# One more level inside two of the seven block products of a SwiGLU up-projection

## The chip, the cores and the metric

The kernel runs on one core of a Trainium2 chip. The metric is the device time in microseconds (us) of one execution, as a median of runs. The page and the trace of the profile come from one profiled execution. Times inside the trace are counted from the first instruction of that execution.

## What is computed

Two layers of a streaming encoder run over 1024 prompt tokens and 32 sample tokens, 1056 together, with 1024 features. Each layer is a mixer with its output projection, then a SwiGLU, then a gated embedding. The part that matters here is the SwiGLU with 2816 hidden features:

```python
def swiglu(x, w1, w3, w2):
    return (jax.nn.silu(x @ w1) * (x @ w3)) @ w2
...
        x = layer_norm(DEEPNORM_ALPHA * x + mix, w['ln1_g'][i], w['ln1_b'][i])
        x = layer_norm(DEEPNORM_ALPHA * x + swiglu(x, w['w_ff1'][i], w['w_ff3'][i], w['w_ff2'][i]),
                       w['ln2_g'][i], w['ln2_b'][i])
        x = x + (ple[i] @ w['w_ple'][i]) * jax.nn.sigmoid(x @ w['w_ple_gate'][i])
```

Everything is float32. A product of two float32 operands is made of three TensorE passes: each operand is split into a high part and a rest (`Weights.split`: ScalarE writes the high part, L88, VectorE the rest, L89), and high by high, rest by high and high by rest are added in PSUM.

## The kernel before

Per layer, `tail` makes the output projection, the first layer norm and group 0 of the hidden features. `up` (L899) makes groups 1 to 10. `final` (L1174) multiplies by w2, and `embed` follows.

A group is 256 hidden features, which is two tiles of 128 columns of w1 and of w3. In `up` each of these two weight matrices is taken as 2 by 2 blocks (feature half by output tile), the activations as 2 by 2 blocks (feature half by token half, 528 tokens), and the product is made by seven block products of sums instead of eight (Winograd's form of Strassen's method). `ops` names the seven activation operands: 1, 2, 3 and 4 lie in the tiles xh and xl, and 5, 6, 7 are the tiles t1, t2, t3, all of them split. Operand 4 is made in place. One block product (`product`, L980) is 4 feature tiles by 3 passes by 2 token quarters, so 24 matmuls of 128 by 128 weights on 264 columns (L989).

`quad` (L1021) runs the seven products of one weight matrix and group in the order 1, 2, 6, 5, 7, 3, 4, in tiles `q` of two PSUM banks each, four of them. ScalarE copies out a first result (`copy`, L1005), VectorE adds later ones onto it (`add`, L1008), `act` applies Silu on ScalarE (L1019) or multiplies by the gate on VectorE (L1017), and `keep` (L895) sends the hidden group to DRAM. Group 1 goes by another order that is not touched.

The weights come through the class `Weights`, a generator in the order of use: SyncE issues the load of a raw tile (L79, two buffers), VectorE makes the sums (`sub`, L94), and each item is split into half of a tile `w` (four buffers). `get` hands out an item and then has the next ones made, until four units are ahead. The instructions are put in order for each engine by a scheduler from that program order.

At the end of `up` the operand tiles are reused for the operands of `final`: hidden blocks and w2. `behind` loads t2 after product 6 of the last matrix, t3 and t1 after its product 7, and the rest, into xh and xl too, is loaded when `final` begins (L1108, L1111). `final` runs seven products again, in the order 1, 7, 6, 4, 5, 2, 3. Each runs over the 11 groups j with 24 matmuls per j (L1202), and from product 7 on it needs sums that VectorE makes in place (L1147). The residual, the tile `stream`, lies in SBUF all the while. It is read by `block_sums` at the start of `up` and written by `final` when its product 1 ends (L1212).

## Time and profile before

| what | before |
|---|---|
| median of three runs | 2317.38 us (2315.13 to 2317.8) |
| time of the profiled execution | 2315.55 us |
| span of its trace | 2313.8 us |
| mean granted TensorE clock | 0.997 of full speed |
| TensorE matmul, weight load | 99%, 98% of the span |
| VectorE, ScalarE | 68%, 43% of the span |

The time of the profiled execution is its span and 1.75 us around it. Busy shares are means over all stages, and the stages differ. Matmul ends are modelled, so a share near 100% says that the engine never ran dry and not how fast it was.

### The profile page before, as it was taken

The page shows a single profiled execution, that of the slowest core. Times are in us where ns is not written, and L with a number is a line of the kernel's source. Part 1 is how long each engine was busy: PE and PEld are TensorE (multiplying, and loading weights), DVE is VectorE, ACT ScalarE, POOL GpSimd, SP SyncE. Part 2 cuts the span into 40 slices and gives each one's busy share as a digit, 9 for nine tenths or more (in the row PEclk, how much of TensorE's full clock was granted, in tenths as well). Part 3 has the DMA queues.
Part 4 walks back from the last instruction along what each step waited for, and adds up shares of the span by engine and source line. Part 5 has one row for each costly group of instructions (what it writes and reads, how often), then busy time and mean ns, then how long its engine had stood idle before and what let it go on. Part 6 is the DMA issues. An engine that isn't in the chain of part 4 may idle for free.

```text
span 2313.8 us, 40696 instructions
## 1 busy us (share of the span) xinstructions
PE 2290.7 (99%) x17375; PEld 2257.9 (98%) x17375; DVE 1572.1 (68%) x2436; ACT 1001.5 (43%) x1671; POOL 32.4 (1%) x40
## 2 busy tenths in 40 slices
PE   9999999999999999999999999999999999999998
PEld 8999999999999999999999989899999999999998
DVE  8755797555544878896556774898455554978893
ACT  5432464333333443584543562464333333444582
POOL 0000000000000000000000120000000000000000
PEclk9999999999999999999999999999999999999999
DMA  4113113222223722034212222023221224621132
GB/s 149 48 56 123 44 59 117 69 89 74 84 74 133 252 79 70 28 104 145 74 38 66 92 81 67 27 74 109 85 74 66 93 74 159 238 86 42 47 99 95
DMA packets 84377, 207.35 MB, mean 90 GB/s; under 512 B 10236, under 2 KB 19652, under 8 KB 84196
## 3 DMA queue, kind: packets, MB, share of 16 engines
q1 hardware_dynamic: 83428, 204.07, 26.5%
q8 instruction: 136, 2.23, 0.4%
q10 hardware_dynamic: 768, 0.68, 0.1%
q14 instruction: 45, 0.37, 0.0%
HBM read 171.57 MB, written 33.16 MB: 88 GB/s over the span
## 4 chain that ended last, share of the span: by engine, by line
PE 91%; DVE 5%; DMA 2%; ACT 1%; issue 1%; POOL 0%; SPq 0%; ACTq 0%; POOLq 0%
PE q L989 37%; PE q L1202 20%; PE q L1330 8%; PE mm L228 6%; PE mm L229 6%; PE mm L230 6%; PE q L1309 2%; PE mm L638 1%; PE mm L639 1%; PE mm L640 1%; DVE bf L94 1%; DMA raw<-w 1%; DVE w L89 1%; PE ms L774 1%; DMA raw<-w_out 1%
## 5 line engine op out<-in xcount | busy, mean ns | idle before, releaser
L1202 PE MATMUL q<-w 128*128 128x264 f32 x3696 | 457.5, 285 | 0.0
L1202 PEld LDWEIGHTS q<-w 128*128 128x128 f32 x3696 | 456.4, 188 | 0.3
L88 ACT ACTIVATE w<-raw 128x512 fp32r<-128x512 f32 (+2 forms) x246 | 185.8, 774 | 223.8 <-issue 76.6
L989 PE MATMUL q<-xhin,w 128*128 128x264 f32 x1664 | 270.9, 284 | 0.6 <-ACT u L392 0.6
L89 DVE TENSOR_TENSOR w<-raw,w 128x512 fp32r<-128x512 f32 (+2 forms) x246 | 213.1, 881 | 54.5 <-ACT w L88 54.2
L89 DVE TENSOR_TENSOR w<-bf,w 128x512 fp32r<-128x512 f32 (+1 forms) x250 | 167.2, 692 | 107.3 <-ACT w L88 106.5
L88 ACT ACTIVATE w<-bf 128x512 fp32r<-128x512 f32 (+1 forms) x250 | 148.4, 628 | 196.9 <-PE q L989 79.5
L989 PEld LDWEIGHTS q<-xhin,w 128*128 128x128 f32 x1664 | 230.3, 188 | 1.2 <-ACT u L392 0.8
L989 PE MATMUL q<-xhgate,w 128*128 128x264 f32 x1280 | 207.8, 284 | 0.5 <-ACT xhgate L962 0.5
L228 PE MATMUL mm<-xhgate,w 128*128 128x384 f32 (+1 forms) x576 | 188.7, 328 | 5.4 <-ACT xhgate L322 4.7
L229 PE MATMUL mm<-xhgate,w 128*128 128x384 f32 (+1 forms) x576 | 187.6, 326 | 0.0
L230 PE MATMUL mm<-xlgate,w 128*128 128x384 f32 (+1 forms) x576 | 186.7, 325 | 0.8 <-DVE xlgate L323 0.8
L989 PEld LDWEIGHTS q<-xhgate,w 128*128 128x128 f32 x1280 | 177.2, 188 | 0.7 <-ACT xhgate L962 0.7
L989 PE MATMUL q<-xlin,w 128*128 128x264 f32 x832 | 169.6, 285 | 0.3 <-DVE xlin L963 0.3
L1330 PE MATMUL q<-xhgate,w 128*128 128x264 f32 x1024 | 167.1, 285 | 0.0
L1330 PEld LDWEIGHTS q<-xhgate,w 128*128 128x128 f32 x1024 | 142.0, 188 | 0.3
L228 PE MATMUL mm<-xhin,w 128*128 128x384 f32 (+1 forms) x384 | 127.1, 332 | 6.3 <-ACT xhin L322 5.5
L989 PE MATMUL q<-xlgate,w 128*128 128x264 f32 x640 | 130.0, 285 | 0.3 <-DVE xlgate L963 0.3
L989 PEld LDWEIGHTS q<-xlin,w 128*128 128x128 f32 x832 | 128.8, 188 | 0.7 <-DVE xlin L963 0.5
L229 PE MATMUL mm<-xhin,w 128*128 128x384 f32 (+1 forms) x384 | 125.4, 327 | 0.6 <-DVE w L89 0.6
L230 PE MATMUL mm<-xlin,w 128*128 128x384 f32 (+1 forms) x384 | 125.0, 327 | 0.1
L989 PE MATMUL q<-t2sum,w 128*128 128x264 f32 x960 | 124.2, 285 | 0.0
(333 smaller groups left out, 4215.1 us busy)
## 6 DMA issues: line engine op xcount, KB each, us to landing
raw<-w SPq DMA_DIRECT2D x116, 512.0 KB, 3.6
hidden<-c SPq DMA_DIRECT2D x44, 528.0 KB, 3.0
raw<-w_gate SPq DMA_DIRECT2D x32, 512.0 KB, 3.6
raw<-w_in SPq DMA_DIRECT2D x16, 512.0 KB, 3.8
raw<-w_out SPq DMA_DIRECT2D x16, 512.0 KB, 3.6
xhdown<-hidden SPq DMA_DIRECT2D x12, 528.0 KB, 7.8
t2down<-hidden SPq DMA_DIRECT2D x8, 528.0 KB, 3.8
t3down<-hidden SPq DMA_DIRECT2D x8, 528.0 KB, 3.7
```

The costliest lines, as they stand in the source:

```text
L88: self.nc.scalar.activation(hi, x, AF.Copy)
L89: self.nc.vector.tensor_tensor(lo, x, hi.bitcast(F32), op=ALU.subtract)
L94: self.nc.vector.tensor_tensor(t, a, b, op=op)
L228: nc.tensor.matmul(ps, wh, xh, start=first, stop=False)
L229: nc.tensor.matmul(ps, wl, xh, start=False, stop=False)
L230: nc.tensor.matmul(ps, wh, xl, start=False, stop=last)
L638: nc.tensor.matmul(o, xh, hi[:, s], start=k == 0, stop=False)
L639: nc.tensor.matmul(o, xh, lo[:, s], start=False, stop=False)
L989: nc.tensor.matmul(ps[:, a, :TH // 2], w[q][:, ks], x[r][:, k, a * TH // 2:(a + 1) * TH // 2], start=not add and k == 0 and j == 0, stop=k ...
L1202: nc.tensor.matmul(ps[m][:, a, :TH // 2], v[q][:, ms], x[r][:, a * TH // 2:(a + 1) * TH // 2], start=j == 0 and n == 0, stop=j == NG - 1 a ...
L1309: nc.tensor.matmul(ps[:, b, :TH // 2], w[q][:, o:o + P], pe[k][r][:, t * TH + b * TH // 2:t * TH + (b + 1) * TH // 2], start=k == 0 and i ...
L1330: nc.tensor.matmul(ps[:, b, :TH // 2], w[q][:, ks], token_half((self.xh, self.xl), k, t, b)[r], start=k == 0 and i == 0, stop=k == KD - 1 ...
```

## The change

In groups 3 to 10 of both layers the products 2 and 4 are no longer made for w1 and w3 apart. The two weight blocks that multiply the same operand, one of w1 and one of w3, are taken side by side as one matrix of 256 columns, and this product goes by one more level of the same seven-product form. Its blocks are 2 feature tiles by 128 columns by 264 tokens, and a product of the inner level (`one`) is 2 by 3 passes, so 6 matmuls of 264 columns. The inner level of product 2 runs within the w1 matrix of a group and that of product 4 within the w3 matrix, in four pieces between the outer products (`within`, `some`). Their results are added to the hidden tiles in pieces of 264 columns.

The outer order becomes 1, inner, 5, 6, 3, 7 in these groups, and 1, 2, 5, 6, 3, 7, 4 in group 2. The weight sums of the inner level are made from a load of its own (`_inner`). Its activation sums are made once per layer, in eight steps that are spread over the last matrix of group 2 and the first of group 3 (`inner`). They lie in the place of `stream`. So `stream` is written to DRAM when `up` begins and read back when it ends. In `up`, PSUM has three tiles `q` and two single banks, `ia` and `ib`. The hidden group goes to DRAM block by block (`keep_block`). `product` is cut in two (`blocks` holds the matmuls) without a change to them.

```diff
@@ -35,6 +35,8 @@
...
+INNER = (2, 4)
...
+            elif kind == "set":
+                yield from self._set(key, *src)
...
+    def _set(self, key, src, order, inner):
+        r0, r1 = (self.raw(v) for v in src)
+        a11, a12, a21, a22 = (r[:, h * 512:(h + 1) * 512] for r in (r0, r1) for h in range(2))
+        sums = {}
+        for i in order:
+            if i == "in":
+                yield from self._inner(*inner)
+                continue
+            if callable(i):
+                i()
+                continue
+            if i == 5:
+                sums[5] = self.sub(a21, a22, ALU.add)
+            elif i == 6:
+                sums[6] = self.sub(sums[5], a11)
+            elif i == 3:
+                sums[3] = self.sub(a12, sums[6])
+            elif i == 7:
+                sums[7] = self.sub(a11, a21)
+            x = {1: a11, 2: a12, 4: a22}.get(i)
+            yield key + (i,), 1, self.split(self.half(), sums[i] if x is None else x)
...
+    def _inner(self, key, src):
+        nc, (raw, own), rest = self.nc, self.extra, self.rest
+        for i, v in enumerate(src):
+            nc.sync.dma_start(out=raw[:, i, :], in_=v)
+        a11, a12, a21, a22 = (raw[:, i, h * 256:(h + 1) * 256] for i in range(2) for h in range(2))
+        x, y = self.temp(512), self.temp(512)
+        s1, s2, s3, s4 = (v[:, h * 256:(h + 1) * 256] for v in (x, y) for h in range(2))
+        for out, a, b, op in (
+            (s1, a21, a22, ALU.add), (s2, s1, a11, ALU.subtract), (s3, a11, a21, ALU.subtract),
+            (s4, a12, s2, ALU.subtract),
+        ):
+            nc.vector.tensor_tensor(out, a, b, op=op)
+        def place():
+            return self.place()[:, :, 0:1024].rearrange("p q (i c) -> p q i c", i=2)
+        own = own if key[3] == INNER[0] else place()
+        self.split(own.rearrange("p q i c -> p q (i c)"), raw.rearrange("p i c -> p (i c)"))
+        sum_ = place()
+        for i, v in enumerate((x, y)):
+            self.split(sum_[:, :, i, :], v)
+        self.rest = rest
+        cut = lambda t, i, h: [t[:, q, i, h * 256:(h + 1) * 256] for q in range(2)]
+        yield key, 2, {
+            1: cut(own, 0, 0), 2: cut(own, 0, 1), 4: cut(own, 1, 1),
+            5: cut(sum_, 0, 0), 6: cut(sum_, 0, 1), 7: cut(sum_, 1, 0), 3: cut(sum_, 1, 1),
+        }
...
-def plan(a, steps, ple):
+def levels(w, g):
+    j = 2 if w == 1 else 4
+    if j not in INNER or g == 2:
+        j = None
+    forms = [1, *(["in"] if j else [2] * (g == 2 or 2 not in INNER)), 5, 6, 3, 7]
+    if 2 not in INNER and "in" in forms:
+        forms.insert(1, 2)
+    if g == 2 or 4 not in INNER:
+        forms.append(4)
+    for i, at in ((2, (3, 2)), (4, (1, 3))):
+        if i in INNER and at == (w, g):
+            for n, f in enumerate((5, 6, 3, 7)):
+                forms.insert(forms.index(f) + 1, (i, n))
+    return j, forms
...
         for g in range(2, NG):
-            blocks("all", g)
+            for w in (1, 3):
+                j, forms = levels(w, g)
+                src = None
+                if j:
+                    o = [a[f"w{v}_{layer}"][2 * g + (j == 4)][:, 512:1024] for v in (1, 3)]
+                    src = ("in", layer, g, j), o
+                forms = [i if i == "in" or type(i) is int else (lambda i=i, layer=layer: inner(layer, *i)) for i in forms]
+                order.append(("set", (layer, w, g), ([a[f"w{w}_{layer}"][2 * g + i] for i in range(2)], forms, src)))
...
                     self.tp = stack.enter_context(tc.tile_pool(name=f"t{layer}", bufs=1, reuse_waits="tile"))
+                    with tc.tile_pool(name=f"psu{layer}", bufs=1, space=PSUM, reuse_waits="tile") as self.psum:
+                        self.psum_bufs = {"q": 3, "ia": 1, "ib": 1}
+                        self.up(layer)
                     self.psum = stack.enter_context(
                         tc.tile_pool(name=f"psb{layer}", bufs=1, space=PSUM, reuse_waits="tile")
                     )
                     self.psum_bufs = {"q": 4}
-                    self.up(layer)
                     self.final(layer)
                     self.embed(layer)
...
         self.begin(layer)
+        for k in range(0, KD, 2):
+            nc.sync.dma_start(out=self.resid[:, k:k + 2, :], in_=self.stream[:, k:k + 2, :])
         last = self.block_sums(self.stream, t1, t2, t3, t4)
...
+        self.inside, self.sh = {}, [self.pair(t, layer, "all") for t in "sc"]
         for g in range(2, NG):
-            s = self.pair("s", layer, g)
-            self.quad((layer, 1, g), s, None, AF.Silu)
-            h = self.pair("c", layer, g)
-            self.quad((layer, 3, g), h, s, step=behind if g == NG - 1 else None)
-            self.keep(layer, g, h)
+            for w in (1, 3):
+                self.mixed(layer, w, g, behind if (w, g) == (3, NG - 1) else None)
+        self.stream = self.const.tile([P, KD, T], F32, tag="stream", name=f"stream{layer}b", bufs=1)
+        self.acc = [self.stream[:, :, t0:t0 + n] for t0, n in CH]
+        for k in range(0, KD, 2):
+            nc.sync.dma_start(out=self.stream[:, k:k + 2, :], in_=self.resid[:, k:k + 2, :])
+    def inner(self, layer, i, step):
+        nc, w, q, x = self.nc, self.w, TH // 2, self.ops[i]
+        if not self.inside:
+            t = self.inner_sums = self.const.tile([P, 32, q], F32R, tag="stream", name=f"inner{layer}", bufs=1)
+            raw = self.tp.tile([P, 1024], F32, tag="rawx", name=f"rawx{layer}", bufs=1)
+            own = t[:, 24:32, :].rearrange("p (q b) t -> p q (b t)", q=2)[:, :, 0:1024]
+            w.extra = raw.rearrange("p (i c) -> p i c", i=2), own.rearrange("p q (i c) -> p q i c", i=2)
+        if step == 0:
+            n, t = INNER.index(i), self.inner_sums
+            t1, t2, t3 = (
+                [t[:, 12 * n + 4 * j + 2 * r:12 * n + 4 * j + 2 * r + 2, :] for r in range(2)] for j in range(3)
+            )
+            own = [[v[:, k:k + 2, h * q:(h + 1) * q] for v in x] for k in (0, 2) for h in range(2)]
+            self.inside[i] = {1: own[0], 2: own[2], 3: own[3], 4: own[1], 5: t1, 6: t2, 7: t3}
+        of = self.inside[i]
+        b11, b12, b21, b22, t1, t2, t3 = (of[n] for n in (1, 4, 2, 3, 5, 6, 7))
+        out, terms = (
+            (t3, (b22, b12, ALU.subtract)), (t2, (t3, b11, ALU.add)), (t1, (b12, b11, ALU.subtract)),
+            (b12, (b21, t2, ALU.subtract)),
+        )[step]
+        u, v, op = terms
+        s = w.temp(TH).rearrange("p (k t) -> p k t", k=2)
+        nc.vector.tensor_tensor(s, u[0].bitcast(F32), v[0].bitcast(F32), op=op)
+        nc.vector.tensor_tensor(s, s, u[1].bitcast(F32), op=ALU.add)
+        nc.vector.tensor_tensor(s, s, v[1].bitcast(F32), op=op)
+        nc.scalar.activation(out[0], s, AF.Copy)
+        nc.vector.tensor_tensor(out[1], s, out[0].bitcast(F32), op=ALU.subtract)
...
+    def mixed(self, layer, w, g, behind):
+        dst, (s, h) = self.sh[w == 3], self.sh
+        gate, func = (None, AF.Silu) if w == 1 else (s, AF.Copy)
+        j, forms = levels(w, g)
+        todo = iter(self.within(layer, j, g)) if j else iter(())
+        two, four = 2 not in forms, 4 not in forms
+        def made(i, ps=None):
+            if behind:
+                self.w.ahead = min(self.w.AHEAD, len(forms) - 1 - forms.index(i)) if i in (5, 6) else self.w.AHEAD
+            (v,) = self.w.get((layer, w, g, i))
+            ps, add = (self.quads(), False) if ps is None else (ps, True)
+            self.blocks(ps, v, self.ops[i], add)
+            if behind:
+                behind(i)
+            return ps
+        def some():
+            next(todo, None)
+        def finish(at, ps=None):
+            self.act(dst, at, gate, func, ps)
+            if w == 3:
+                self.keep_block(layer, g, at)
+        u = made(1)
+        if two and w == 3:
+            self.add(dst, (0, 0), u)
+            finish((0, 0))
+        else:
+            self.copy(dst, (0, 0), u)
+        if not two:
+            self.add(dst, (0, 0), made(2))
+            finish((0, 0))
+        some()
+        v = made(5)
+        self.copy(dst, (1, 1), v)
+        some()
+        made(6, u)
+        self.copy(dst, (0, 1), u)
+        some()
+        made(3, v)
+        self.add(dst, (0, 1), v)
+        finish((0, 1))
+        some()
+        if j:
+            self.act(s, {2: (0, 0), 4: (1, 0)}[j], None)
+        made(7, u)
+        self.add(dst, (1, 1), u)
+        finish((1, 1))
+        if not four:
+            made(4, u)
+            finish((1, 0), u)
+        elif w == 1:
+            self.copy(dst, (1, 0), u)
+        else:
+            self.add(dst, (1, 0), u)
+            finish((1, 0))
...
+    def within(self, layer, j, g):
+        nc, q, d, x = self.nc, TH // 2, self.sh, self.inside[j]
+        m, t = {2: (0, 0), 4: (1, 0)}[j]
+        (w,) = self.w.get(("in", layer, g, j))
+        def bank(tag):
+            return self.bank(tag)[:, :q]
+        def one(ps, i, add):
+            for k in range(2):
+                for c, (p, r) in enumerate(((0, 0), (1, 0), (0, 1))):
+                    nc.tensor.matmul(
+                        ps, w[i][p][:, k * P:(k + 1) * P], x[i][r][:, k, :],
+                        start=not add and k == 0 and c == 0, stop=k == 1 and c == 2, skip_group_check=add,
+                    )
+            self.passed(6 * q)
+        def to(a, b, ps, new=False):
+            o = d[a][:, m, t * TH + b * q:t * TH + (b + 1) * q]
+            if new:
+                nc.scalar.activation(o, ps, AF.Copy)
+            else:
+                nc.vector.tensor_tensor(o, o, ps, op=ALU.add)
+        u = bank("ia")
+        one(u, 1, False)
+        to(0, 0, u)
+        v = bank("ib")
+        one(v, 2, False)
+        to(0, 0, v)
+        yield
+        v = bank("ib")
+        one(v, 5, False)
+        to(1, 1, v, True)
+        one(u, 6, True)
+        to(0, 1, u)
+        yield
+        one(v, 3, True)
+        to(0, 1, v)
+        one(u, 7, True)
+        to(1, 1, u)
+        yield
+        one(u, 4, True)
+        to(1, 0, u, True)
+        yield
...
+    def keep_block(self, layer, g, at):
+        m, t = at
+        self.nc.sync.dma_start(
+            out=self.hidden[layer][:, m, t, g, :], in_=self.sh[1][:, m, t * TH:(t + 1) * TH]
+        )
```

## Rows read from the trace of the kernel before

**Rows 1.** The page's first part: busy time, share of the span and instructions.
```profile
span 2313.8 us, 40696 instructions
PE 2290.7 (99%) x17375; PEld 2257.9 (98%) x17375; DVE 1572.1 (68%) x2436; ACT 1001.5 (43%) x1671; POOL 32.4 (1%) x40
```
**Rows 2.** The chain of waits from 340 to 860 us: start, length, what.
```profile
353.85 4.24 DMA raw<-w
...
360.75 1.20 DVE w L89 x2
361.95 1.23 DVE s L1008 x2
...
377.36 372.42 PE q L989 x3049
749.78 110.23 PE q L1202 x894
```
**Rows 3.** Windows: length, busy us and instructions of each engine, PEclk, DMA share, GB/s.
```profile
360.00:370.00 10.00, 10.00 (x84) 10.00 (x84) 10.00 (x18) 4.47 (x8) 0.00 (x0) 1.00 0.33 104
...
379.50:749.50 370.00, 370.00 (x3033) 370.00 (x3032) 189.34 (x294) 127.27 (x220) 0.00 (x0) 1.00 0.27 88
749.50:784.00 34.50, 34.50 (x282) 34.50 (x281) 26.06 (x42) 15.13 (x27) 0.00 (x0) 1.00 0.97 354
784.00:846.00 62.00, 62.00 (x505) 62.00 (x504) 50.70 (x83) 26.24 (x46) 0.00 (x0) 1.00 0.31 102
...
1589.00:1958.70 369.70, 369.70 (x3031) 369.70 (x3030) 188.92 (x293) 126.89 (x219) 0.00 (x0) 1.00 0.26 88
```
**Rows 4.** Waits of TensorE from 1548 to 2055 us: total, times, longest.
```profile
PE q L989 <- ACT xhgate L962: 0.5, 1, 0.5
PE q L989 <- DVE xlgate L963: 0.3, 1, 0.3
```
**Rows 5.** VectorE's groups from 461 to 502 us, one group of hidden features.
```profile
L89 DVE TENSOR_TENSOR w<-bf,w 128x512 fp32r<-128x512 f32 x8 | 5.3, 689 | 5.1 <-ACT w L88 5.0
L89 DVE TENSOR_TENSOR w<-raw,w 128x512 fp32r<-128x512 f32 x6 | 4.0, 686 | 0.0
L1017 DVE TENSOR_TENSOR c<-c,s 128x528 f32<-128x528 f32 x4 | 2.8, 706 | 0.1
...
L94 DVE TENSOR_TENSOR bf<-raw 128x512 f32<-128x512 f32 x2 | 1.4, 693 | 7.2 <-DMA raw<-w 7.2
```
**Rows 6.** VectorE's timeline from 330 to 385 us: start, length, instruction.
```profile
339.26 0.45 DVE L885 TENSOR_TENSOR c<-c,mm 128x288 f32<-128x288 f32 x1
339.63 1.94 DVE L94 TENSOR_TENSOR bf<-stream 128x528 f32<-128x528 f32 x3
```
**Rows 7.** Windows of 5 us at the end of `up` and the start of `final`.
```profile
755.00:760.00 5.00, 5.00 (x43) 5.00 (x42) 3.18 (x6) 3.36 (x6) 0.00 (x0) 1.00 0.80 286
...
775.00:780.00 5.00, 5.00 (x43) 5.00 (x42) 4.96 (x9) 1.78 (x3) 0.00 (x0) 1.00 1.05 395
...
785.00:790.00 5.00, 5.00 (x43) 5.00 (x42) 4.79 (x9) 2.22 (x4) 0.00 (x0) 1.00 0.00 0
```
**Rows 8.** SyncE's queue in the timeline, 690 to 1020 us.
```profile
738.08 0.38 SPq L1108 DMA_DIRECT2D t2down<-hidden  x1
...
743.96 0.37 SPq L1108 DMA_DIRECT2D t3down<-hidden  x1
...
749.34 1.59 SPq L895 DMA_DIRECT2D hidden<-c  x2
750.98 0.52 SPq L1111 DMA_DIRECT2D t1down<-w  x1
758.18 0.33 SPq L1111 DMA_DIRECT2D t1down<-hidden  x1
758.61 0.90 SPq L1108 DMA_DIRECT2D xhdown<-hidden  x2
```
**Rows 9.** VectorE's timeline from 736 to 800 us.
```profile
749.82 0.71 DVE L1017 TENSOR_TENSOR c<-q,s 128x528 f32<-128x528 f32 x1 [0.52 <-PE q L989]
...
764.60 1.33 DVE L1147 TENSOR_TENSOR xhdown<-xhdown 128x528 f32<-128x528 f32 x2 [0.97 <-DMA xhdown<-hidden]
```

More of the change, by code (lines that the diff above doesn't have):

```diff
@@ L59, in __init__ @@
     def __init__(self, nc, pool, order):
-        self.nc, self.pool, self.count, self.rest = nc, pool, 0, None
+        self.nc, self.pool, self.count, self.rest, self.ahead = nc, pool, 0, None, self.AHEAD
         self.made, self.items, self.temps, self.temp_bufs = [], self._make(order), None, 5
@@ L74, in half, with raw_place @@
         return t
+    def raw_place(self):
+        self.count += 1
+        return self.pool.tile([P, T], F32, tag="raw", name=f"raw{self.count}", bufs=2)
     def raw(self, src):
-        self.count += 1
-        raw = self.pool.tile([P, T], F32, tag="raw", name=f"raw{self.count}", bufs=2)[:, :src.shape[1]]
+        raw = self.raw_place()[:, :src.shape[1]]
         self.nc.sync.dma_start(out=raw, in_=src)
@@ L127, in _make, with prefetch @@
                 yield own(a22)
-    def prefetch(self, n=AHEAD):
+    def _set(self, key, src, order, inner):
[44 more added lines that the diff above has]
+        }
+    def prefetch(self, n=None):
+        n = self.ahead if n is None else n
         while sum(m[1] for m in self.made) < n:
@@ L145, in get, with plan @@
         return out
-def plan(a, steps, ple):
+def levels(w, g):
[12 more added lines that the diff above has]
+    return j, forms
+def plan(a, steps, ple, inner):
     order = []
@@ L255, in build @@
             ring = ctx.enter_context(tc.tile_pool(name="ring", bufs=1, side="right"))
-            self.w = Weights(nc, ring, plan(a, self.steps, self.ple))
+            self.w = Weights(nc, ring, plan(a, self.steps, self.ple, self.inner))
             self.const = const
@@ L292, in build @@
             self.spill = dram.tile([P, KD, T], F32, name="spill")
+            self.resid = dram.tile([P, KD, T], F32, name="resid")
             self.acd = dram.tile([72, P], F32, name="acd")
@@ L980, in product, with blocks @@
     def product(self, key, i, ps=None):
-        nc, x = self.nc, self.ops[i]
         (w,), add = self.w.get(key), ps is not None
         ps = ps if add else self.quads()
+        self.blocks(ps, w, self.ops[i], add)
+        return ps
+    def blocks(self, ps, w, x, add):
+        nc = self.nc
         for k in range(4):
@@ L993, in product @@
         self.passed(12 * TH)
-        return ps
     @staticmethod
```

## The prediction

> **What bounds the kernel now.** I read the page's busy line first. TensorE and its weight loads are busy nearly all the time, VectorE two thirds and ScalarE under half [rows 1]. A busy TensorE on the page only means that it never ran dry, so I looked for what the end hangs on, in the chain of waits. Around the change it has two long pieces that are TensorE alone: 372.42 us for 3049 matmuls of `up` and 110.23 us for 894 of `final` [rows 2]. That is 0.1222 and 0.1233 us for one matmul of 264 columns. The waits of TensorE over the second layer's `up` and half of its `final` come to 0.8 us [rows 4]. So in this stretch a matmul left out is time left out, as long as the other engines still deliver.
>
> They have room of different size. In the windows by stage, groups 2 to 10 show VectorE busy 189.34 of 370.00 us and ScalarE 127.27 [rows 3]: 51% and 34%. The second layer repeats this within half a per cent [rows 3]. Ahead of this stretch the chain runs over VectorE and loads of raw weights [rows 2], and there a window shows VectorE busy 10.00 of 10.00 us while TensorE does all its 84 matmuls [rows 3]. So VectorE can be packed full for some ten us without hurting TensorE, but has nothing left there. The third thing to see is the DMA: from the end of `up` to 784 us it is busy 97% of the time at 354 GB/s [rows 3], at best 395 GB/s, and it falls to nothing only after 785 us [rows 7].
>
> **What is removed.** Two outer products in w1 and two in w3 are 4 x 24 = 96 matmuls in a group. Two inner products of seven times 6 matmuls are 84. So 12 matmuls less for each of 8 groups and 2 layers, 192 in all. They have the shape of those that stay, and each of them loads a weight tile of its own before and after, so the price is the one of the chain: 192 x 0.1222 = **23.5 us**. The Trainium skill, "TensorE: Matmul & The Clock Gate", section "Back-to-back issue gap", gives columns over 2.4 GHz and 2.5 ns, which is an estimate of 112.5 ns here and would make it 21.6 us. The chain shows 9% more for a matmul, and the sum keeps that.
>
> **VectorE in a group.** Instructions of 512 and 528 columns follow each other in 0.60 to 0.62 us [rows 2], one of 288 columns from PSUM in 0.37 us (339.26 to 339.63) [rows 6]. By the line through these, 256 or 264 columns cost 0.34 and 1024 about 1.12. A group has now 14 splits, 8 sums, 6 additions from PSUM and 4 gate products, 32 instructions or about 19.5 us. The window shows 189.34 / 9 = 21.0 us [rows 3], 1.08 times that. After the change there are 10 outer splits, 2 of 1024 and 4 of 512 for the inner level, 8 sums of 512 and 8 of 256, 6 + 10 additions (the 10 of half width), 4 gate products: 6.0 + 4.6 + 4.8 + 2.7 + 3.7 + 3.4 + 2.5 = 27.7 us, times 1.08 = 30 us. TensorE's group shrinks from 41.1 to 324 x 0.1222 = 39.6 us, so VectorE goes from 51% to 76%. ScalarE, at 127.27 / 220 = 0.58 us each, goes from 24 to about 32 instructions a group, under half busy. Both are hidden behind TensorE as means. A rule speaks against the small additions: the Trainium skill, "VectorE: DVE Perf Modes", section "The TRN2 errata", gives 120 cycles and the columns at 0.96 GHz for an operand from PSUM, so an estimate of 0.40 us for 264 columns. By that the group would be 0.6 us more. The 288-column row shows 0.37, and either way 76% hardly moves.
>
> What can be lost is in the order. VectorE's idle time in a group is mostly waiting: 7.2 us on two loads of raw weights and 5.0 on ScalarE [rows 5]. The inner level adds a second load, issued behind the first, and such a wait holds the additions queued behind it. The single bank `ib` is read by VectorE after one inner product and written again after one outer product, 24 x 0.1222 = 2.9 us later. A wait of 3.6 us (half of the 7.2) standing ahead of that addition would cost TensorE up to 3.6 + 0.34 - 2.9 = 1.0 us, in up to 32 matrices. Bounds 0 to 32 us. Nearest to it are the packed stretch and the waits [rows 3, 4], where TensorE lost under a microsecond. I take 1 us for both layers.
>
> **The start of `up`.** Writing `stream` out is 8 x 1056 x 128 x 4 bytes = 4.33 MB, 11 to 12 us of DMA at 395 to 354 GB/s [rows 3, 7]. It goes ahead of raw weights on SyncE's queue, and the chain has such a load at 353.85 us, 4.24 us long [rows 2]. But `stream` is final before the block sums that read it at 339.63 us [rows 6], and the DMA share in the window at 360 us is 0.33 [rows 3], so the write should be over when that load comes. 0 to 3 us a layer, taken 0.5.
>
> **Group 2 and the activation sums.** Eight steps of four VectorE instructions are 8 x 4 x 0.615 = 20 us of VectorE in two matrices that last 40 us, on top of about 23 us. Full, but group 2's first matrix still has idle time before it. If VectorE falls behind, TensorE waits as far as the slack of some 3 us is used up: 0 to 5 us a layer, taken 1. In group 2 product 4 follows product 7 into the same bank, and VectorE's addition stands between. Such an addition starts 0.04 us after the matmuls of a product end (749.78 to 749.82) and lasts 0.71 [rows 2, 9], so 0.75 us, twice a layer. Another matrix's product may fill it. 0 to 1.5, taken 1.
>
> **The end of `up`.** Here the 4.33 MB come back, into a stretch where the DMA is full. Three things move. First, product 7 was third from the end and is now last, so the loads of t3 and t1, issued from 743.96 us, 5.8 us before the change to `final` at 749.78 [rows 2, 8], wait for the end of `up`. The loads of t2 come after product 6, which now has 24 + 24 + 18 matmuls behind it, so 8.1 us before the end where it was 11.7 (738.08) [rows 8]. Second, the read back takes 11 to 12 us. Third, something is gained: the queue stood from 751.5 to 758.18 us on the load of a hidden block that `keep` had only issued at 749.34 [rows 8], and block by block that one is written early.
>
> Two orders are possible on SyncE. If the read back goes as soon as its place is free (the inner sums are last used ahead of product 3, 54 matmuls or 6.6 us before the end), it fills the DMA until about +9 us, counted from the end of `up`. The first pair of blocks and weights in t3, 1.06 MB at 354 to 395 GB/s, lands at about +12, and after 2.5 us of splits (8 instructions on two engines) serves j = 4 at +14.5. TensorE wants that at 4 x 2.93 = +11.7: a stall of **3 us**. If the loads of t3 and t1 go first, 3.2 MB and the read back end near +20, then come a rest of 0.8 MB and 1.6 MB for the first pair of product 7, landing at +26. VectorE then has eight instructions for it and four evacuations of product 1, 7.4 us, so +33.4 against product 7's start at 264 x 0.1222 = +32.3. Before, the first of these sums started at 764.60 us, +14.8 [rows 9], so this cover of 17 us is what the read back eats. A stall of 0 to 3 us. Bounds: 0 if the queue overlaps better, 12 if all of the read back is paid. I take 3 us a layer, and 0.5 for the start of `final` with its later t2 loads (0 to 3).
>
> The Trainium skill, "DMA: Bandwidth & Descriptors", section "Specifications", gives a limit of about 358 GB/s for HBM and one core. By that the read back is an estimate of 12.1 us, and the stall 1 us longer. The best window shows 395 GB/s [rows 7], which is above that limit.
>
> **The sum.** Losses a layer: 0.5 + 1 + 1 + 3 + 0.5 = 6, and 1 in the groups: 13 us for both layers. 23.5 - 13 = 10.5 us less. The profiled execution took 2315.55 us, which gives 2305. The median of the runs stands 1.8 us above it, so I predict **2306 us** for the median. Its own range, with half or one and a half of the losses, is 2300 to 2313.
>
> **Rivals.** *Nearly everything is hidden*: the losses stay under 4 us, and the time is 2294 to 2299. For it speaks that TensorE lost under 1 us where VectorE was full [rows 3, 4]; against it that the DMA has no idle time at the end of `up` to hide 4.33 MB [rows 7].
>
> *The read back is paid*: both layers lose 10 to 12 us at the change to `final`, the gain is gone, and the time is 2313 to 2321. For it speaks the full DMA, against it the 17 us of cover before product 7.
>
> *VectorE comes to set the pace in the groups*, which ends on the other side: waits on loads and on ScalarE stay (12.2 us of a group [rows 5]) and come on top of 30 us of work, 42.2 us against TensorE's 39.6. Sixteen groups at 2.6 us are 42 us, so 42 - 23.5 = some 18 us slower, 2335, and 2325 to 2345 around it. It decides from 10.5 / 32 = 0.33 us of stall a matrix. Against it: these waits come mostly from VectorE being early, and shrink when it is busy.
>
> That the matmuls aren't saved is excluded by the count.
>
> **Chances.** Forecast 45%, nearly all hidden 24%, read back paid 15%, VectorE at the pace 16%. A measurement of this kernel can tell about 0.2%, here 4.6 us, from no change, so faster is below 2312.7. The forecast lies there but for some 3 points, the first rival altogether, the second with 2 points: 68% faster. The same is 3 + 12 = 15%, and slower 1 + 16 = 17%. The range of 8 in 10 takes in the first three cases and the near part of the fourth, 2294 to 2325.
>
> **What would show it.** Right: 17183 matmuls on the page; windows of a group of 39.6 to 40.5 us with VectorE at 70 to 80%; TensorE's waits short and near the start of `final`, on ScalarE's splits of t3 or VectorE's sums; DMA full until about 45 us past `up`. Wrong: waits of TensorE on inner additions in every group (VectorE at the pace), or a single gap of 8 us and more before product 7 or j = 4 (read back paid), or none at all (hidden). The prediction falls with the ready times at the end of `up`, which hang on an order on SyncE that the trace before cannot show.

## The result and the profile after

The changed kernel takes 2303.08 us (median of 6 runs, 2300.83 to 2303.82) where the kernel before took 2317.59 beside it (6 runs, 2315.13 to 2319.16). The ratio is 0.9937, interval 0.9927 to 0.9947: 14.5 us less, where 11 were forecast. A second series of the same kernel, told below with the experiments, gives 2297.34 beside 2316.82 before, ratio 0.9916, interval 0.9899 to 0.9932, 19.5 us less. Both intervals lie wholly below 1, and they overlap each other.

The page's first part, against [rows 1]:

```profile
span 2298.6 us, 41143 instructions
...
PE 2270.4 (99%) x17183; PEld 2236.8 (97%) x17183; DVE 1736.9 (76%) x2820; ACT 1060.7 (46%) x1783; POOL 32.5 (1%) x40
```

The 192 matmuls are gone, and yet the count of all instructions is 447 higher. VectorE has 384 more and went from 68% to 76% of the span. TensorE is still the engine that never rests. Windows of the changed kernel, columns as in [rows 3]; the first is one group of hidden features, the others lie at the start of `final`:

```profile
467.10:506.70 39.60, 39.60 (x327) 39.60 (x326) 28.66 (x53) 16.77 (x30) 0.00 (x0) 1.00 0.33 109
742.00:747.00 5.00, 3.74 (x19) 3.77 (x20) 4.79 (x8) 1.15 (x2) 0.00 (x0) 0.67 0.95 330
...
777.00:782.00 5.00, 5.00 (x43) 5.00 (x42) 4.83 (x9) 3.20 (x6) 0.00 (x0) 1.00 0.96 368
782.00:787.00 5.00, 5.00 (x43) 5.00 (x42) 5.00 (x9) 2.39 (x5) 0.00 (x0) 1.00 0.06 22
1942.00:1947.00 5.00, 3.73 (x30) 3.76 (x31) 4.80 (x8) 1.15 (x2) 0.00 (x0) 1.00 0.96 301
```

From the first matmul of a group to that of the next are 39.55 us, where it was 41.01 (both counted in the traces). That is 1.46 us less, or 23.4 us in the sixteen groups. TensorE is busy throughout, and VectorE at 72%. The DMA stays full until 782 us, 39 us past the start of `final` at 743.26. Something is lost at that start: TensorE is busy for 3.74 of 5.00 us, and its granted clock falls to 0.67 in layer 0 and not at all in layer 1. All waits of TensorE over `up` and half of `final`, layer 0 (320 to 860 us) and then layer 1 (1500 to 2060 us), against [rows 4]; L1448 is `final`, L1236 an outer product of `up`:

```profile
PE q L1448 <- DVE c_all L1254: 2.2, 1, 2.2
PE q L1236 <- DVE xlin L1205: 0.2, 1, 0.2
...
PE q L1448 <- ACT w L93: 2.1, 1, 2.1
PE q L1236 <- DVE xlgate L1205: 0.3, 1, 0.3
...
PE q L1236 <- DVE c_all L1254: 0.2, 1, 0.2
```

There is one wait of some 2 us a layer, and the others are of 0.2 to 0.3 us, near the start of `up`. The chain of waits puts the long one at the first matmul of `final` in both layers (start, length, what):

```profile
733.02 4.79 DMA t2down<-hidden
737.84 1.18 ACT w L93 x2
...
741.89 1.24 DVE c_all L1254 x2
743.26 116.76 PE q L1448 x933
...
1934.55 7.47 DMA t2down<-w
...
1942.04 1.16 ACT w L93 x2
...
1943.27 116.76 PE q L1448 x945
```

In layer 0 the last thing waited for is VectorE's addition, in layer 1 ScalarE's split of a tile of t2. There the additions end at 1943.12 and the split at 1943.20, so both stand in the way.

Where the time came from is read stage by stage, from the first matmul of each stage to that of the next (us, worked out from the starts in the three traces; the last column is the same changed kernel in the second series):

| stretch | before | changed | changed, again |
|---|---|---|---|
| start to the first matmul of the convolution's projections | 58.8 | 61.3 | 59.7 |
| from there to `up` | 280.2 | 280.2 | 279.5 |
| `up`, layer 0 | 410.6 | 401.8 | 401.8 |
| `final`, layer 0 | 229.9 | 231.4 | 230.0 |
| end of `final` to the next `up` | 567.8 | 566.1 | 566.2 |
| `up`, layer 1 | 411.5 | 402.5 | 402.7 |
| `final`, layer 1 | 229.8 | 229.9 | 229.9 |

By the forecast's price an `up` should fall by 96 x 0.1222 = 11.7 us, to 398.9 and 399.8. It falls by 8.8 to 9.0, so 2.7 to 2.9 us a layer are lost in it, most of it the one wait. The first profile also lost 1.5 us in `final` of layer 0, where the clock fell, and 2.5 us at the kernel's start, which the change doesn't touch. The stretch from `final` to the next `up` lies anywhere between 566.1 and 567.8 us in the profiles of this document, so its 1.7 us are not put down to the change.

### The profile page after: what moved, and what is told of

Read it like the earlier page. It is cut to its first block, busy times and chain, and to the rows that moved or that the text cites. A ratio compares the mean times of both kernels' runs of the same rounds, so it can differ in the third digit from the quotient of the medians.

```text
span 2298.6 us, 41143 instructions
## 1 busy us (share of the span) xinstructions
PE 2270.4 (99%) x17183; PEld 2236.8 (97%) x17183; DVE 1736.9 (76%) x2820; ACT 1060.7 (46%) x1783; POOL 32.5 (1%) x40
## 4 chain that ended last, share of the span: by engine, by line
PE 88%; DVE 7%; DMA 2%; ACT 2%; issue 1%; SPq 0%; POOL 0%; POOLq 0%; ACTq 0%
PE q L1236 28%; PE q L1448 20%; PE q L1576 8%; PE mm L314 6%; PE mm L315 6%; PE mm L316 6%; PE ia L1153 4%; PE ib L1153 3%; PE q L1555 2%; DVE bf L99 1%; PE mm L727 1%; PE mm L728 1%; PE mm L729 1%; DVE w L94 1%; DMA raw<-w 1%; PE ms L863 1%
## 5 line engine op out<-in xcount | busy, mean ns | idle before, releaser
L1448 PE MATMUL q<-w 128*128 128x264 f32 x3696 | 459.1, 286 | 4.3 <-DVE c_all L1254 2.2
L1448 PEld LDWEIGHTS q<-w 128*128 128x128 f32 x3696 | 457.8, 189 | 4.9 <-ACT w L93 4.7
L94 DVE TENSOR_TENSOR w<-raw,w 128x512 fp32r<-128x512 f32 (+2 forms) x182 | 171.2, 946 | 97.7 <-ACT w L93 97.5
L94 DVE TENSOR_TENSOR w<-bf,w 128x512 fp32r<-128x512 f32 (+1 forms) x314 | 207.0, 687 | 37.7 <-ACT w L93 37.3
L1236 PE MATMUL q<-xhin,w 128*128 128x264 f32 x1152 | 188.3, 285 | 0.6 <-ACT u L481 0.6
L1576 PE MATMUL q<-xhgate,w 128*128 128x264 f32 x1024 | 167.1, 285 | 0.0
L1236 PEld LDWEIGHTS q<-xhin,w 128*128 128x128 f32 x1152 | 159.5, 188 | 1.5 <-ACT u L481 0.8
L1576 PEld LDWEIGHTS q<-xhgate,w 128*128 128x128 f32 x1024 | 142.0, 188 | 0.3
L1236 PE MATMUL q<-xhgate,w 128*128 128x264 f32 x768 | 125.3, 285 | 0.3 <-ACT xhgate L1204 0.2
L1236 PE MATMUL q<-t3sum,w 128*128 128x264 f32 x960 | 124.3, 285 | 0.0
L1236 PE MATMUL q<-t1sum,w 128*128 128x264 f32 x960 | 124.0, 285 | 0.0
L1236 PE MATMUL q<-t2sum,w 128*128 128x264 f32 x960 | 123.6, 284 | 0.0
L1236 PEld LDWEIGHTS q<-t1sum,w 128*128 128x128 f32 x960 | 120.3, 189 | 0.0
L1236 PEld LDWEIGHTS q<-t3sum,w 128*128 128x128 f32 x960 | 120.0, 189 | 0.0
```

Source lines behind the costliest of these rows:

```text
L94: self.nc.vector.tensor_tensor(lo, x, hi.bitcast(F32), op=ALU.subtract)
L1236: nc.tensor.matmul(ps[:, a, :TH // 2], w[q][:, ks], x[r][:, k, a * TH // 2:(a + 1) * TH // 2], start=not add and k == 0 and j == 0, stop=k ...
L1448: nc.tensor.matmul(ps[m][:, a, :TH // 2], v[q][:, ms], x[r][:, a * TH // 2:(a + 1) * TH // 2], start=j == 0 and n == 0, stop=j == NG - 1 a ...
L1576: nc.tensor.matmul(ps[:, b, :TH // 2], w[q][:, ks], token_half((self.xh, self.xl), k, t, b)[r], start=k == 0 and i == 0, stop=k == KD - 1 ...
```

## The experiments

The theory after the result: the saving is worth its full price, VectorE and the read back are hidden, and the losses are the wait at the start of `final`, made by the new order of the last matrix: 5, 6, 3, 7. Product 7 is last, so its additions and the loads behind them come last. Rivals: the read back or the write of `stream` still costs (a), VectorE's extra work costs in the groups (b), or the frame of the change (wider tiles, the order, the spill) costs something that the saving hides (c).

**The frame alone, and half of the saving.**

```diff
-INNER = (2, 4)
+INNER = ()
```

> No product goes by the inner level; the new order of the products, three tiles q, block-wise sending of the hidden groups, and the writing out and reading back of the residual stay. Theory A (what was lost of the 23.5 us lies at the end of the up-projection, in the later loads and in the read back, and not in the inner level): TensorE's work is that of before, and the time is 2318 to 2324 us, with a wait of TensorE at the start of the down-projection. Theory B (the loss comes with the inner level: VectorE's additional work, the short matmul groups in the two single banks): no wait there, and 2316 to 2318 us, the time of before.

```diff
-INNER = (2, 4)
+INNER = (2,)
```

> Only product 2 goes by the inner level, product 4 as before, so 96 matmuls less instead of 192. If each matmul left out is worth 0.122 us and nothing else changes with the inner level, half of the gain of the matmuls is missing: 2303.1 + 11.7 = 2314.8 us, less what the end of the up-projection gains by product 4 coming last again (0 to 5 us): 2310 to 2315. If the inner level itself costs VectorE's time in each group, less is lost by leaving half of it out, 2306 to 2310.

Measured: 2325.77 us (1.0042, 1.0027 to 1.0057), above the range that either theory gave, and 2314.08 us (0.9991, 0.9982 to 1.0000). From the frame to one inner product are 11.7 us. The step on to both can only be taken across series, each against its own kernel before: 12.6 us to the first series, 17.5 to the second. Each step is 96 matmuls, 11.7 us by the price, but the waits change along with it, so the two steps agree with the price and don't prove it. The 1.46 us of a group, above, is the direct reading: 12 matmuls at 0.122 us. The frame costs 9.7 us against the kernel before, more than the 4 to 9 us that the full change loses. But its wait is another one: with no inner products in between, product 4 of the last matrix directly follows 7 into the same bank, and VectorE's addition stands behind the splits of t2. TensorE waits 2.2 us in layer 0 and 3.7 in layer 1, and the clock falls each time (windows of the frame alone):

```profile
752.00:757.00 5.00, 4.07 (x21) 4.07 (x22) 2.71 (x5) 1.09 (x2) 0.00 (x0) 0.68 1.02 366
1965.00:1970.00 5.00, 3.20 (x14) 3.21 (x15) 3.58 (x6) 1.59 (x3) 0.00 (x0) 0.55 1.03 371
```

Rival (c) is thus true in its sign, but the cost can't be carried over as it stands to the full change.

**The order of the last matrix.** It alone is set to 1, inner products, 6, 5, 7, 3, with the loads of t2 a product earlier. The core of it:

```diff
+    if (w, g) == (3, NG - 1):
+        forms = [1, "in", 6, 5, 7, 3]
...
-            if i == 5:
+            if i in (5, 6) and 5 not in sums:
```

> In the last matrix of each layer the order is 1, inner, 6, 5, 7, 3, so that the loads behind products 6 and 7 go out some 6 us (t2) and 3 us (t3) earlier. Theory A (the wait at the start of the down-projection is for splits of t2, which is loaded too late, and the clock falls behind it): both waits of 2.2 us go and the stretch of low granted clock in the first layer too, 2297 to 2300 us. Theory C (the read back fills the DMA, and a wait must come somewhere): the wait moves to a later operand of the down-projection, 2301 to 2304 us.

Measured: 2293.40 us (2292.29 to 2293.78), ratio 0.9900 (0.9884 to 0.9917), less than either theory expected. That is faster than the kernel before and than the first series of the changed kernel; the interval of the second series overlaps. `up` takes 400.3 and 400.5 us, `final` 229.8 twice. Its waits of TensorE, layer 0 and then layer 1, show that the one at `final` is gone:

```profile
PE q L1256 <- ACT xhin L1224: 0.5, 1, 0.5
...
PE q L1256 <- DVE c_all L1274: 0.5, 1, 0.5
```

Its SyncE queue issues t2 388.1 us after the start of `up` (338.28), where the changed kernel did so after 391.5 (733.02 and 341.49): 3.4 us earlier. The read back goes last:

```profile
726.39 0.38 SPq L1374 DMA_DIRECT2D t2down<-hidden  x1
...
735.15 0.36 SPq L1374 DMA_DIRECT2D t3down<-hidden  x1
...
741.30 2.43 SPq L1047 DMA_DIRECT2D stream0b<-resid  x4
```

`final` begins here before VectorE has added the last product of `up`, which is now 3 (a line of the chain, and one of VectorE's timeline):

```profile
738.75 225.06 PE q L1468 x1825
...
738.97 0.69 DVE L1274 TENSOR_TENSOR c_all<-c_all,q 128x528 f32<-128x528 f32 x1
```

So a last product doesn't hold `final` up as such. It does when it lies in the bank that `final` takes first, as product 7's seems to do in the changed kernel, where `final` starts 0.14 us after its additions. In this run they end at 737.2, 1.4 us ahead. In the kernel before, too, `final` had begun at 749.6 when VectorE took up its last product at 749.82 [rows 9]. The four tiles of `final` are laid out anew over those of `up` in the changed kernel. No run kept its order and gave `final` another first bank, so that rival to the new order as a remedy is untested.

**Without the traffic of the stream.** The residual is set to zero on GpSimd in place of the write and the read back.

```diff
-            nc.sync.dma_start(out=self.resid[:, k:k + 2, :], in_=self.stream[:, k:k + 2, :])
...
-            nc.sync.dma_start(out=self.stream[:, k:k + 2, :], in_=self.resid[:, k:k + 2, :])
+            nc.gpsimd.memset(self.stream[:, k:k + 2, :], 0.0)
```

> The residual is neither written out nor read back; GpSimd sets its tile to zero in place of the read back, so the residual is left out of the second half of each layer. Theory A (later loads behind products 6 and 7): the waits at the start of the down-projection stay, 2301 to 2304 us. Theory C (the 4.33 MB read back in a full DMA): they go, and the time falls by 4 to 6 us to 2297 to 2299.

The result then lacks the residual. Measured: 2299.37 us, 0.9931 (0.9916 to 0.9945), between the two series of the changed kernel. The waits at `final` stay, 1.6 and 1.8 us, and `up` takes 401.4 and 402.4. In the first profile of the changed kernel they were 2.2 and 2.1, but in the second, with the traffic, 1.6 and 1.8 as well. So the wait exists without the traffic, and no part of it can be put down to the traffic.

**Other buffers for the loads.** The three loads at the end take other places, so that t2 comes a product earlier while product 7 stays last.

```diff
-            for n in {6: (1,), 7: (2, 3)}.get(p, ()):
+            for n in {5: (1,), 6: (2,), 7: (3,)}.get(p, ()):
...
-        tags = "t2", "t3", "t1"
+        tags = "t1", "t2", "t3"
```

> The changed kernel with its order of products, but the first operands of the down-projection are loaded into the place of t1 (free after product 5), the next into that of t2 (after 6) and the last into that of t3 (after 7), so the first loads go out 4.4 us earlier and nothing else moves. If the wait at the start of the down-projection comes from loads that land late, it goes: 2295 to 2299 us. If it comes from product 7 being last (VectorE still has two additions and two gate products for its bank), it stays: 2300 to 2303 us.

Measured: 2298.77 us, 0.9928 (0.9913 to 0.9942), and a wait of 1.5 us in each layer. VectorE's and TensorE's timelines of layer 0 (start, length, instruction, idle before it):

```profile
741.67 1.32 DVE L1254 TENSOR_TENSOR c_all<-c_all,q 128x528 f32<-128x528 f32 x2 [0.65 <-PE q L1236]
...
743.14 3.03 PE L1448 MATMUL q<-w 128*128 128x264 f32 x23 [1.50 <-DVE c_all L1254]
```

VectorE was idle, began the moment the last matmuls of product 7 were over, and `final` still had to wait for two additions of 0.6 us to free the bank. In the changed kernel the same additions stand behind four splits of the late t2:

```profile
739.97 1.29 DVE L94 TENSOR_TENSOR w<-t2down,w 128x512 fp32r<-128x512 f32 x2
741.18 0.70 DVE L1263 TENSOR_TENSOR c_all<-c_all,s_all 128x528 f32<-128x528 f32 x1
741.80 1.31 DVE L1254 TENSOR_TENSOR c_all<-c_all,q 128x528 f32<-128x528 f32 x2
...
737.98 3.08 PE L1236 MATMUL q<-t3sum,w 128*128 128x264 f32 x24
743.26 4.92 PE L1448 MATMUL q<-w 128*128 128x264 f32 x26 [2.20 <-DVE c_all L1254]
```

So two things stand in the way, one behind the other: late loads, and product 7 last in the bank that is wanted. With the first taken away 1.5 us of wait stay for the second. The late loads account for the rest, 0.7 and 0.6 us in the first profile and 0.1 and 0.3 in the second. In time that share isn't seen: `up` takes 401.8 and 402.4 us here, as in the changed kernel, and the interval of the ratio overlaps those of both series. Only the order of the earlier run (1, inner, 6, 5, 7, 3) took away both.

**More work on VectorE.** On top of that order, 5 and then 8 instructions of 528 columns, which nothing uses, in each of the two inner matrices of a group (`n` runs over 5 or 8):

```diff
+                self.nc.vector.tensor_tensor(t, t if n else x, x, op=ALU.max)
```

> The version of e3_last_order with 5 additional VectorE instructions of 528 columns on each of the 32 matrices with an inner level, whose results nobody uses: 6.2 us more for VectorE in each of the 16 groups, so it goes from 72% (28.7 of 39.6 us) to 88%. If VectorE's waits are mostly earliness, they shrink and nothing is seen: 2293 to 2297 us. If its waits of a group before (12.2 us) stay on top of its work, VectorE sets the pace and each microsecond shows: 2293 + 16 x 6 = near 2390 us.

> As e6_vector_plus_10 with 8 additional instructions a matrix, 9.9 us a group: VectorE at 97%. Earliness: the waits that are left begin to show, 2300 to 2330 us. VectorE at the pace: near 2450 us.

Measured: 2294.79 us (0.9909, 0.9893 to 0.9926) and 2302.38 us (0.9942, 0.9927 to 0.9957), against 2293.40 for the order alone. Windows of 40 us in the groups, of the first and of the second:

```profile
500.00:540.00 40.00, 40.00 (x330) 40.00 (x329) 36.90 (x67) 17.51 (x32) 0.00 (x0) 1.00 0.32 107
```

```profile
500.00:540.00 40.00, 40.00 (x328) 39.85 (x327) 39.13 (x70) 17.34 (x30) 0.00 (x0) 1.00 0.32 107
```

With VectorE at 92% in its window `up` takes 400.4 and 401.6 us, at most 1.1 more than with the order alone. At 98% it takes 403.7 and 404.6, 3.4 and 4.1 more. The change stands at 72%, so rival (b) is out, with room for some ten instructions more in a group.

**The read back twice.** On top of the order, a copy of `resid` in DRAM beside each read back.

```diff
+            nc.sync.dma_start(out=self.spare[:, k:k + 2, :], in_=self.resid[:, k:k + 2, :])
```

> The version of e3_last_order in which each piece of the residual that is read back is also copied from DRAM to DRAM, 4.33 MB more on the same queue at the same place. If the read back is hidden with a few microseconds of cover to spare, the additional 11 us or more of DMA make product 7 of the down-projection wait by 5 to 15 us a layer: 2303 to 2325 us. If the DMA has room for it, no change: 2292 to 2296 us.

Measured: 2293.95 us, 0.9906 (0.9892 to 0.9921). It missed its aim: the copies were issued at 336 to 350 us, as soon as `resid` was written, and not at the end of `up`. It shows something else: 4.33 MB more at the start of `up` cost nothing, as `up` took 399.8 and 399.7 us.

**The same order without the traffic, with more of it, and the changed kernel again.** The first drops write and read back as above (residual left out). The second adds, at the end of `up` and on GpSimd's queue:

```diff
+        for t in (1, 0):
+            nc.gpsimd.dma_start(out=self.spare[:, t], in_=self.hidden[layer][:, 1, t])
```

> The last matrix of `up` in the order 1, inner, 6, 5, 7, 3, and the residual is neither written to DRAM nor read back (its tiles are set to zero on GpSimd, so the residual is left out of the result). If the write and the read back are hidden whole in that order: 2292 to 2295 us, as with the traffic. If they still cost something at the start of `up` or ahead of `final`: 2288 to 2291.

> The same order, with the traffic, and two copies of hidden blocks from DRAM to DRAM on GpSimd's queue at the end of `up` in each layer, which nothing reads. If the read back was hidden because the DMA has room to spare before product 7 of `final` needs its tiles: 2292 to 2296. If the room is only a few us: product 7 of `final`, or the additions at the end of `up`, wait for loads, 2298 to 2320, with TensorE waits on DMA or on splits of late loads 20 to 50 us into `final`.

> The changed kernel again, beside the two others: 2300 to 2304, with waits of about 2 us at the start of each `final`, and its first matmul of the convolution's projections at 59 to 61.5 us, by chance.

Measured: 2293.52 us (0.9901, 0.9886 to 0.9916), 2320.27 us (1.0016, 1.0007 to 1.0026) and 2297.34 us (0.9916, 0.9899 to 0.9932). Without traffic the order takes what it took with it, so the read back is hidden whole. With 5.95 MB more the gain is gone: `final` takes 242.7 and 242.9 us instead of 229.8, 13 us a layer. Windows of that run, where `final` began at 738.7:

```profile
763.00:768.00 5.00, 3.22 (x27) 3.00 (x25) 0.00 (x0) 0.00 (x0) 0.00 (x0) 1.00 1.03 379
768.00:773.00 5.00, 0.00 (x0) 0.00 (x0) 0.00 (x0) 0.00 (x0) 0.00 (x0) 0.78 0.91 339
773.00:778.00 5.00, 2.66 (x10) 2.38 (x11) 1.88 (x3) 1.21 (x2) 0.00 (x0) 0.50 1.04 403
778.00:783.00 5.00, 5.00 (x32) 5.00 (x31) 4.77 (x9) 2.44 (x4) 0.00 (x0) 0.69 1.05 403
```

TensorE waits 9.1 us for the last pair of product 1, whose hidden block lands 29.2 us after its issue at 744.8. With the order alone the same load lands after 13.4 us, at 758.0, and its pair is wanted at 738.7 + 9 x 2.93 = 765.1, less 2 us of splits. So the cover behind the read back is 763 - 758 = 5 us in this order. By the wait it is 6.7: the load came 29.2 - 13.4 = 15.8 us later and TensorE waited 9.1. What comes on top is paid, first as a wait and then once more as a lower clock. The Trainium skill, "DMA: Bandwidth & Descriptors", section "Specifications", limits HBM and one core to about 358 GB/s, which would be an estimate of 16.6 us for 5.95 MB. The delay of 15.8 us is near that, yet two of the four windows show 403 GB/s, above that limit.

## Why the prediction was right, point by point

**The saving** was right: 23.5 us forecast, and 16 x 1.46 = 23.4 us in the groups. A group takes 39.55 us, the low end of the forecast's 39.6 to 40.5. The Trainium skill, "TensorE: Matmul & The Clock Gate", section "Back-to-back issue gap", gives its formula for an isolated matmul; by it a group would be 324 x 112.5 ns, an estimate of 36.5 us. The trace shows 39.55, so the price from the chain was the better one.

**VectorE in a group**: 30 us forecast, 28.66 measured, 72% for 76%. The loss of 1 us for the waits in groups was nil. The waits on raw weights that were feared shrank from 7.2 us [rows 5] to 0.5, with 0.4 on the new load beside them, and those on ScalarE from 5.0 to 3.7, as argued under the third rival: they came from VectorE being early. VectorE's waits in the same group of the changed kernel:

```profile
DVE s_all L1164 <- PE ia L1153: 3.7, 2, 2.3
DVE w L94 <- ACT w L93: 3.7, 2, 3.2
...
DVE bf L99 <- DMA raw<-w: 0.5, 1, 0.5
```

**The start of `up`** (0.5 a layer) and **group 2 with product 4** (2 a layer) were sized too high. No wait is long enough to stand out, but the starts of the matmuls show them: where one follows the last after more than 0.18 us instead of 0.122, what is over can be added up. Where group 1 takes operand 4, near 380 us, it is 0.5 and 1.0 us (1.0 and 1.5 in the second profile), and it was 0.5 and 1.3 before, so no cost is clear. In group 2 and at the start of group 3 it is 0.4 to 0.8 us a layer, and nothing before. The scheduler put matmuls of another product between 7 and 4, as the prediction allowed. In the frame alone, where the last matrix had nothing to put there, the same place cost 2.2 and 3.7 us.

**The read back** was mis-sized: 3 us a layer were taken, and nothing was paid. All waits in the changed kernel from 743 to 800 us, of any engine:

```profile
ACT w L93 <- PE q L1448: 25.3, 13, 6.7
DVE w L94 <- ACT w L93: 13.2, 8, 4.1
ACT w L93 <- DVE xldown L1393: 3.4, 4, 1.8
...
PE q L1448 <- DVE c_all L1254: 2.2, 1, 2.2
```

None of them is for the DMA. The splits wait for TensorE to free their places, which means that the loads are there. The order on SyncE was neither of the two forecast ones but between them: t1 was not held back to the end of `up` but went ahead of t2, and of the read back one part of four went before t3 and three behind it:

```profile
728.64 0.38 SPq L1354 DMA_DIRECT2D t1down<-hidden  x1
...
733.02 0.37 SPq L1354 DMA_DIRECT2D t2down<-hidden  x1
...
735.03 1.04 SPq L1045 DMA_DIRECT2D stream0b<-resid  x1
...
742.34 0.39 SPq L1354 DMA_DIRECT2D t3down<-hidden  x1
...
745.92 2.14 SPq L1045 DMA_DIRECT2D stream0b<-resid  x3
...
749.08 2.92 SPq L1354 DMA_DIRECT2D xhdown<-hidden  x2
```

With that neither t3 nor product 7's tiles came late: VectorE starts the sums for product 7 at 767.62, +24.4, where the second of the two orders had their loads landing only at +26. That the DMA is full for 39 us was right, and that a full DMA must then cost was not. The reserve is 5 to 7 us in the order of the third run and was not measured in the changed kernel. So the second rival was not far off.

**The start of `final`** was mis-sized the other way: 0.5 us a layer taken, 2.2 and 2.1 measured (1.6 and 1.8 in the second series), and in the first profile 1.5 us more in layer 0 by the clock. The step spoke of later t2 loads alone, which are the smaller share. It left out that product 7, now last, holds a bank that `final` wants until VectorE has added it, behind those same splits. The sign forecast for the wait (near the start of `final`, on ScalarE's splits or VectorE's sums) did show, though for t2 and not t3.

**The sum**: the losses, forecast at 13 us, were 23.5 - 14.5 = 9.0 by the medians of the first series and 4.0 by those of the second. By its own terms the forecast is 2317.38 - 10.5 = 2306.9 us, so 2307 and not 2306. The result of the first series lies in the forecast's own range, 2300 to 2313; that of the second lies in the range of the rival in which nearly everything is hidden. The errors of the terms are larger than that of the sum: some 11 us of forecast loss did not come, 3.4 to 5.8 came at the start of `final` where 1 was forecast, and in the first profile the kernel's start added 2.5 that have nothing to do with the change. That the total came so close is in part luck.

**Still open**: whether another first bank for `final` would do what the new order does, how much of its wait the late loads really cost, and the start of the kernel (below). The order of the third run is faster than the changed kernel by its stages (1.5 and 2.0 us in `up`, 1.5 and 2.2 against the second series); the intervals of the two ratios (0.9884 to 0.9917, and 0.9899 to 0.9932 in the second series) touch.

## What to carry to other kernels

When work is saved on the engine that sets the pace, price it by the chain's own duration, and then look for losses at the change of stages and not in the steady groups. There, ask of the last product in the old stage two things at once: which bank the new stage needs from it, and what stands ahead of its additions in VectorE's queue. In this kernel a full DMA was no loss as long as the load that is wanted first landed before TensorE came to it; what the splits wait for tells which it is, TensorE or the DMA.

## What the runs showed of the hardware

A wait of TensorE can cost more than itself. In these profiles the waits of 2.2 us (changed kernel, layer 0; frame alone, layer 0), 3.7 and 9.1 us were followed by a stretch of lower granted clock, 0.67, 0.68, 0.55 and 0.50 in windows of 5 us; 0.50 is the lower level, 1.2 GHz. Waits of 1.5 to 2.1 us at the start of `final` were not: there the windows show 1.00 (changed kernel in layer 1 and in the second series, without traffic, other buffers, one inner product). At the kernel's start, next, a wait of 1.8 us was, so its length alone does not tell. In the changed kernel the wait of 2.2 us in layer 0 cost 1.5 us once more.

The kernel's start is not the same each time. The second half of `w_in` landed for ScalarE's split at 6.62 us in the kernel before and at 7.62 in the changed one, though the code there is the same (windows from 10 to 20 us, of before and of the changed kernel):

```profile
10.00:20.00 10.00, 10.00 (x59) 10.00 (x58) 8.66 (x12) 7.74 (x12) 0.00 (x0) 1.00 1.07 373
```

```profile
10.00:20.00 10.00, 10.00 (x50) 10.00 (x49) 7.07 (x9) 6.79 (x11) 0.00 (x0) 0.84 1.07 375
```

TensorE waited 1.8 us for it instead of 0.5, and did 9 matmuls less in these 10 us, at a granted clock of 0.84. With the 6 fewer of the first 10 us (16 instead of 22) it is 15 behind. These have 384 columns and follow each other in 0.175 us, so that is 2.6 us, about the 2.5 us between the two starts. In the second series the same kernel waited 1.4 us, kept a clock of 1.00 and was at 59.7. Why the load lands at different times stayed open; it is noise of 2 us that a single profile puts on any change.
